# Four w_down products move from a stand-alone run into the first two Strassen pairs of a two-layer MLP

## The chip, the cores and the metric

The kernel runs on one core of one Trainium2 chip. The metric is device time in microseconds (us), the median of several runs; smaller is better. Traces come from one profiled execution.

## The reference

Two layers, each a token mixer (two kinds of attention with gates) followed by an MLP, on 512 tokens of width 1024 in float32. The change lies in the MLP of each layer:

```python
h = rmsnorm(x, norm_mlp)
return x + jnp.square(jax.nn.relu(h @ w_up)) @ w_down      # w_up 1024x4096, w_down 4096x1024
```

The result is a sum over the 4096 hidden columns, so a part of `w_down` can be applied as soon as its hidden columns are there.

## The kernel before

**Matmuls.** Every float32 operand is split into a rounded part `h` and a rest `lo`. A product with a contraction of 128 is three matmuls: h*h, h*lo, lo*h (lines 212 to 214, and 1195 through `mm`). Weights come from HBM as a tile `raw` (128x1024), ScalarE (ACT) casts it to `wh` (L186), VectorE (DVE) subtracts to get `wl` (L187).

**The MLP** (`mlp`, L912) holds the activations transposed, 128 columns by 512 tokens each, and has four stages:

1. The first 8 of 32 column blocks of `w_up` are multiplied plainly and give `acts[0:8]` (`PLAIN = 8`, L947 to L961).
2. A stand-alone run of w_down products (L963). One such product, a "down", is `down(c, m, w)` (L929): 4 activations by one 128-wide block of `w_down`, 12 matmuls of 512 columns, and one DVE addition into `x[m]` (L933). Downs come from the generator `D` in fixed order, c = 0 to 5 and m = 0 to 7; two successive ones share one `raw` tile from the array `wd2`, so tile k serves downs 2k and 2k+1. There are 48 of them in a layer; 16 stand here.
3. Twelve "units", one for each remaining pair g = 4 to 15 of `w_up` blocks (L975). A unit (`Strassen.unit`, L1203) does its 2x2 block product with seven products instead of eight. Each is 12 matmuls of 256 columns (`product`, L1190). The list in L975 says how many downs may go between a unit's products; the places are after products 1, 3, 5 and 6 (`between`).
4. The last quarter of `w_down` (`wdn`).

**Inside a unit** seven products p0 to p6 use four PSUM banks. p4 is added onto the bank of p2, p5 onto that of p0, p6 onto that of p1. So p4 waits until DVE has read p2 (`sub(y[:, 1], ...)`, shown as L1218), and p6 until DVE has read p1 (`c2`, L1236), which itself needs p4. After that the results go through ACT (ReLU, square, cast: L1259 to L1261) and GpSimd (POOL, L1262) to become two more activations.

**Conversion.** `S.load(g)` (L1157) fetches a pair's two raw tiles, into the buffers tagged `e` for even g and `raw` for odd g, two buffers each. `convert(g)` (L1167) forms four sums (two on POOL, L1176 and L1177; two on DVE, L1181 and L1182) and seven pairs `sh` (ACT, L1185) and `sl` (DVE, L1186), one for each product. Unit g carries along the conversion of pair g+1, and there are 8 buffers for `sh`, so a later `sh` waits for an earlier product to end.

**What sets the order.** Each engine works its own queue strictly in order; a scheduler fixes these queues when the program is built, by program order, readiness and free buffers. DMA loads of weights all go through one in-order queue on SyncE (SP). `order` (L678) lists the order and the buffer tag of the weight loads: a `wd2` tile with c = 0 or 1 (tiles 0 to 7, downs 0 to 15) uses the two `raw` buffers, which odd pairs also use; all later ones use the one buffer `crs`. One weight tile is converted ahead of its use (`ahead`, L199), and only when a `wh` buffer (there are two) is free of the products that read it.

The code that the change touches:

Of the kernel before, what the change touches and what calls it, by code (L numbers as in the profile page):

```python
# [137 lines left out]
def run(*gens):  # L138
    for g in gens:
        for _ in g:  # L140
            pass


class Body:
# [533 lines left out]
    def order(self, l):  # L678

        a = self.a  # L680
        flat = lambda ap: ap.rearrange("p k c -> p (k c)")
        wb = [flat(a["wb"][l, i]) for i in range(32)]
        for c in range(4):
            s = a["wva"][l, c]
            if l == 0 and c == 0:
                yield from ((s[:, j], 512) for j in range(2))
            else:
                yield flat(s), 1024
        yield from ((flat(a["wg2"][l, c]), 576) for c in range(4))
        for i in (0, 1, 2, 3, 8, 9, 4, 5, 6, 7, 10, 12, 13, 11):  # L690
            yield wb[i], 1024
        wo = [[flat(a["wo"][l, f, m]) for m in range(4)] for f in range(2)]
        for m in range(8):
            yield wb[16 + m], 1024
            if m % 2 == 1:
                yield wo[0][m // 2], 1024
            if m in (1, 3):
                yield wb[14 + m // 2], 1024
        yield from ((wb[24 + m], 1024) for m in range(8))
        yield from ((wo[1][m], 1024) for m in range(4))  # L700
        yield from ((flat(a["wout"][l, m]), 1024) for m in range(8))
        yield from ((flat(a["wup"][l, j]), 1024) for j in range(self.PLAIN))
        yield from ((a["wd2"][l, c, m], 1024, *(("crs",) if c > 1 else ())) for c in range(6) for m in range(4))
        yield from ((flat(a["wdn"][l, m]), 1024, *(("crs",) if m == 0 else ())) for m in range(8))

    def layer(self, l, u):
# [205 lines left out]
    def mlp(self, l, x, u, acc, gm):  # L912

        nc, a = self.nc, self.a
        R = None
        pend = []
        acts = []

        def act(ps):
            t = self.t("tmp", [128, T])  # L920
            nc.vector.scalar_tensor_tensor(t, ps, 0.0, R, op0=OP.max, op1=OP.mult)
            h = self.t("oh", [128, T], F32R)
            lo = self.t("ol", [128, T], F32R)
            nc.scalar.activation(t, t, AF.Square)
            nc.scalar.copy(h, t)
            nc.vector.tensor_tensor(lo, t, h.bitcast(F32), op=OP.subtract)
            acts.append((h, lo))

        def down(c, m, w):  # L929

            ps = self.bank()
            yield from self.gemm(ps, w, 4 * (m % 2), acts[4 * c:4 * c + 4], ks=4)
            nc.vector.tensor_add(x[m], x[m], ps)  # L933

        def downs():
            for c in range(6):
                for m in range(8):
                    if m % 2 == 0:
                        w = self.weights(a["wd2"][l, c, m // 2])
                    yield lambda: run(down(c, m, w))  # L940

        S = Strassen(self, l, x, gm)
        D = downs()
        raws = [None] * 16
        g0 = self.PLAIN // 2
        S.load(g0)
        for j in range(self.PLAIN):  # L947
            ps = self.bank()
            w = self.weights(a["wup"][l, j].rearrange("p k c -> p (k c)"))
            run(self.gemm(ps, w, 0, u))  # L950
            if R is None and j == 0:
                pend.append(ps)
                continue
            if R is None:
                R, _ = self.rstd(acc, (self.turn_tag(), self.turn_tag()))
                prep = S.prepare(R)
                for p in pend:
                    act(p)
            act(ps)
            for _ in range(3):  # L960
                next(prep, None)  # L961
        conv = S.convert(g0)
        for i in range(16):  # L963
            next(D)()
            if i < 7:
                next(prep, None)
                next(prep, None)
            elif i == 7:
                run(prep)
            else:  # L970
                next(conv, None)
            if i == 14:
                S.load(g0 + 1)
        run(conv)
        for g, n in zip(range(g0, 16), (0, 0, 3, 3, 4, 4, 4, 4, 4, 4, 2, 0)):  # L975
            S.load(g + 2)
            S.unit(g, D, n, acts)
        u_next = []
        acts = acts[24:]
        if l + 1 < L:  # L980
            acc = []
            self.load_small(l + 1)
            for m in range(8):
                ps = self.bank()
                w = self.weights(a["wdn"][l, m].rearrange("p k c -> p (k c)"))
                run(self.gemm(ps, w, 0, acts))
                nc.vector.tensor_add(x[m], x[m], ps)
                acc = self.sumsq(x[m], acc, m == 7)
                u_next.append(self.make_u(x[m], self.gain[:, 16 * l + 16:16 * l + 24], m))
                nc.scalar.dma_start(self.xs[m], x[m])  # L990
        else:
            self.last(x, acts, a["wdn"][l])
        self.acc = acc
        return u_next
# [305 lines left out]
```

## Time and profile before

| | |
|---|---|
| median of 3 runs | 1565.65 us (1564.94 to 1565.85) |
| the profiled execution's own time | 1566.34 us |
| its span, first to last instruction | 1564.5 us |
| TensorE (PE) busy in the span | 1541.8 us |
| VectorE (DVE) busy | 1079.2 us |
| ScalarE (ACT) busy | 775.3 us |
| GpSimd (POOL) busy | 206.8 us |
| mean granted TensorE clock | 0.994 |

PE counts as busy while matmuls stand in its pipeline. A timeline row has the start and the length in us, the engine, the line, the operation, what it writes and reads, and in brackets how long the engine sat idle before it and on what. A row of the view by windows has, for a stretch of the span, its length, then for PE, PE's weight loads, DVE, ACT and POOL the busy time and the number of instructions, then the granted clock (1.00 is full), the share of the DMA engines, and GB/s.

### The profile page before, as it was taken

To read this page: it belongs to the slowest core of one execution; us is meant where nothing else is said; L and a number is where in the kernel's file an instruction comes from. 1 tells how busy PE (TensorE), PEld (TensorE's weight loads), DVE (VectorE), ACT (ScalarE), POOL (GpSimd) and SP (SyncE) were. 2 spreads that over 40 slices of the span, in tenths; PEclk is the share of its full clock that TensorE was granted. 3 is DMA by queue.
4 is the path that set the end of the run, shared out by engine and by line. 5 is a ranking of instruction groups with operands and counts; after the bars stand their busy time and mean duration, and the time that the engine had idled before them with its cause. 6 is when DMAs were issued, how large, how long until landed. Compare 5 with 4: busy or idle time off the path is not lost. (4 is left out here: it accounts for less than half of the span.)

```text
span 1564.5 us, 22738 instructions
## 1 busy us (share of the span) xinstructions
PE 1541.8 (99%) x8460; PEld 1312.6 (84%) x8460; DVE 1079.2 (69%) x2204; ACT 775.3 (50%) x1455; POOL 206.8 (13%) x177
## 2 busy tenths in 40 slices
PE   9999999999999899999999999999999998999997
PEld 8867888888888899999887688888888888999997
DVE  5687988866478776664646689887574977766643
ACT  6444665543454455444443456555444625545552
POOL 4000000000200332221300000000002013222122
PEclk9999999999999999999999999999999999999998
DMA  7545422143333332322535543222433332333231
GB/s 239 169 134 153 118 82 81 60 131 96 105 94 122 95 95 94 109 81 65 181 109 172 158 129 95 71 78 68 148 95 95 95 121 82 102 101 96 67 96 54
DMA packets 56638, 169.57 MB, mean 108 GB/s; under 512 B 7344, under 2 KB 8112, under 8 KB 56528
## 3 DMA queue, kind: packets, MB, share of 16 engines
q1 hardware_dynamic: 53072, 161.84, 33.8%
q10 hardware_dynamic: 3456, 6.29, 1.2%
q8 instruction: 66, 1.08, 0.3%
q14 instruction: 44, 0.36, 0.1%
HBM read 140.77 MB, written 4.19 MB: 93 GB/s over the span
## 5 line engine op out<-in xcount | busy, mean ns | idle before, releaser
L186 ACT CAST wh<-raw 128x1024 fp32r<-128x1024 f32 (+2 forms) x187 | 192.6, 1030 | 279.1 <-issue 58.5
L187 DVE TENSOR_TENSOR wl<-raw,wh 128x1024 fp32r<-128x1024 f32 (+2 forms) x187 | 226.6, 1212 | 50.9 <-ACT wh L186 50.2
L212 PE MATMUL ps_mm<-uh,wh 128*128 128x512 f32 x512 | 205.2, 401 | 0.0
L214 PE MATMUL ps_mm<-uh,wl 128*128 128x512 f32 x512 | 202.3, 395 | 0.0
L213 PE MATMUL ps_mm<-ul,wh 128*128 128x512 f32 x512 | 202.1, 395 | 0.0
L399 ACT ACTIVATE E<-E,mx 128x128 f32<-128x128 f32 x192 | 108.0, 563 | 82.3 <-DVE mx L398 75.1
L430 ACT CAST pth<-ps_PT 128x512 fp32r<-128x512 f32 x144 | 73.0, 512 | 94.9 <-PE ps_PT L421 94.6
L212 PEld LDWEIGHTS ps_mm<-uh,wh 128*128 128x128 f32 x512 | 96.2, 188 | 26.6 <-issue 10.6
L214 PEld LDWEIGHTS ps_mm<-uh,wl 128*128 128x128 f32 x512 | 96.2, 188 | 20.4 <-issue 0.8
L213 PE MATMUL ps_mm<-ol,wh 128*128 128x512 f32 (+1 forms) x288 | 111.4, 387 | 1.2 <-POOL ol L1262 1.2
L212 PE MATMUL ps_mm<-oh,wh 128*128 128x512 f32 (+1 forms) x288 | 111.8, 388 | 0.0
L214 PE MATMUL ps_mm<-oh,wl 128*128 128x512 f32 (+1 forms) x288 | 111.2, 386 | 0.0
L398 DVE CUSTOM_DVE_ANT_0 E<-ps_S,ct 128x128 f32<-128x128 f32 x192 | 92.3, 484 | 26.5 <-PE ps_S L395 25.2
L213 PEld LDWEIGHTS ps_mm<-ul,wh 128*128 128x128 f32 x512 | 96.5, 188 | 15.1
L1186 DVE TENSOR_TENSOR sl<-s,sh 128x512 fp32r<-128x512 f32 x96 | 80.8, 845 | 35.7 <-ACT sh L1185 35.7
L431 DVE TENSOR_TENSOR ptl<-ps_PT,pth 128x512 fp32r<-128x512 f32 x144 | 85.1, 596 | 27.6 <-ACT pth L430 27.1
L1262 POOL TENSOR_TENSOR ol<-c,oh 128x512 fp32r<-128x512 f32 x48 | 62.7, 1306 | 284.3 <-ACT oh L1261 265.8
L1185 ACT CAST sh<-raw 128x512 fp32r<-128x512 f32 x72 | 44.6, 620 | 100.0 <-PE ps_S L1195 44.2
L253 POOL TENSOR_TENSOR acc<-sq 128x512 f32<-128x512 f32 (+1 forms) x6 | 8.3, 1391 | 594.4 <-DVE wl L187 580.2
L1185 ACT CAST sh<-s 128x512 fp32r<-128x512 f32 x96 | 59.3, 620 | 55.0 <-PE ps_mm L1195 19.2
L421 PE MATMUL ps_PT<-ct,E 128*128 128x128 f32 x480 | 83.0, 273 | 1.4 <-DVE ptl L431 1.4
L421 PEld LDWEIGHTS ps_PT<-ct,E 128*128 128x128 f32 x480 | 60.1, 140 | 14.8 <-DVE ptl L431 4.1
(441 smaller groups left out, 4085.0 us busy)
## 6 DMA issues: line engine op xcount, KB each, us to landing
raw<-wb SPq DMA_DIRECT2D x64, 512.0 KB, 3.3
raw<-wup SPq DMA_DIRECT2D x64, 512.0 KB, 3.6
raw<-wd SPq DMA_DIRECT2D x48, 512.0 KB, 3.6
kd<-hl SPq DMA_DIRECT2D x48, 256.0 KB, 4.6
w<-w SPq DMA_DIRECT2D x32, 256.0 KB, 5.7
q<-hl SPq DMA_DIRECT2D x64, 128.0 KB, 2.9
raw<-wo SPq DMA_DIRECT2D x16, 512.0 KB
raw<-wout SPq DMA_DIRECT2D x16, 512.0 KB, 3.5
```

Source lines behind the costliest of these rows:

```text
L186: nc.scalar.copy(h[:, :n], raw[:, :n])
L187: nc.vector.tensor_tensor(lo[:, :n], raw[:, :n], h[:, :n].bitcast(F32), op=OP.subtract)
L212: mm(ps, h[:, c], xh, start=start and i == 0, stop=False)
L213: mm(ps, h[:, c], xl, start=False, stop=False)
L214: mm(ps, lo[:, c], xh, start=False, stop=stop and i == ks - 1)
L398: nc.vector.tensor_tensor_reduce(e, ps[:, :n], self.mask[:, T - n:], -1.0, BIG, OP.add, OP.min, mx)
L399: nc.scalar.activation(e, e, AF.Exp, bias=mx, scale=-1.0, accum_out=sm[:, i:i + 1])
L421: nc.tensor.transpose(ps[:, j * 128:(j + 1) * 128], E[i][:, b * 128:(b + 1) * 128], self.ident)
L430: nc.scalar.copy(h[:, o:o + n], ps[:, :n])
L431: nc.vector.tensor_sub(lo[:, o:o + n], ps[:, :n], h[:, o:o + n].bitcast(F32))
L1185: nc.scalar.copy(h, src)
L1186: nc.vector.tensor_tensor(lo, src, h.bitcast(F32), op=OP.subtract)
```

## The change

Twelve downs instead of 16 stand in stage 2. The two steps of pair g=4's conversion that went beside each of downs 8 to 15 go two by two beside downs 8 to 11. The load of the second pair (g=5) is asked for at down index 10 instead of 14. Units g=4 and g=5 get two downs each instead of none. The tiles 6 and 7 of `wd2` (downs 12 to 15) move from the tag `raw` to `crs`. From the third unit on, the number of downs done is the same as before. Both layers run this code.

```diff
-        yield from ((a["wd2"][l, c, m], 1024, *(("crs",) if c > 1 else ())) for c in range(6) for m in range(4))
+        yield from ((a["wd2"][l, c, m], 1024, *(("crs",) if 4 * c + m > 5 else ())) for c in range(6) for m in range(4))
...
-        for i in range(16):
+        for i in range(12):
             next(D)()
             if i < 7:
                 next(prep, None)
...
                 run(prep)
             else:
                 next(conv, None)
-            if i == 14:
+                next(conv, None)
+            if i == 10:
                 S.load(g0 + 1)
         run(conv)
-        for g, n in zip(range(g0, 16), (0, 0, 3, 3, 4, 4, 4, 4, 4, 4, 2, 0)):
+        for g, n in zip(range(g0, 16), (2, 2, 3, 3, 4, 4, 4, 4, 4, 4, 2, 0)):
             S.load(g + 2)
             S.unit(g, D, n, acts)
```

## The prediction

> **What bounds the kernel now.** I read the page first, then the waits of PE, then PE's timeline around them, and last a table by windows.
>
> ```profile
> span 1564.5 us, 22738 instructions
> PE 1541.8 (99%) x8460; PEld 1312.6 (84%) x8460; DVE 1079.2 (69%) x2204; ACT 775.3 (50%) x1455; POOL 206.8 (13%) x177
> ```
>
> PE is the bound: 1541.8 of 1564.5 us. The change leaves every matmul in place, so it can only win what PE stands still or runs slowly. In the Strassen units of both layers these five rows of PE's timeline are the only ones with an idle time:
>
> ```profile
> 524.54 0.38 PE L1195 MATMUL ps_mm<-t,sh 128*128 128x256 f32 x1 [0.95 <-DVE y L1218]
> 529.65 0.39 PE L1195 MATMUL ps_O<-b_q,sh 128*128 128x256 f32 x1 [1.38 <-DVE c L1236]
> 542.18 0.39 PE L1195 MATMUL ps_O<-b_q,sh 128*128 128x256 f32 x1 [2.19 <-DVE c L1236]
> 1296.38 0.39 PE L1195 MATMUL ps_PT<-t,sh 128*128 128x256 f32 x1 [1.88 <-DVE y L1218]
> 1313.98 0.58 PE L1195 MATMUL ps_S<-b_q,sh 128*128 128x256 f32 x1 [2.19 <-DVE c L1236]
> ```
>
> All five lie in the first two units of a layer, the ones without downs, at p4 (L1218) or p6 (L1236). Now the windows: the stand-alone downs, the first two units of layer 0, the third and fourth, the eleventh unit, g=14 (two downs), the first two units of layer 1, and three short stretches behind the long waits.
>
> ```profile
> 474.16:517.68 43.52, 43.52 (x193) 36.04 (x192) 34.51 (x50) 15.48 (x22) 5.13 (x4) 1.00 0.34 110
> 517.68:546.05 28.37, 23.85 (x181) 23.23 (x180) 22.07 (x31) 15.61 (x29) 9.53 (x7) 0.94 0.37 113
> 546.05:584.00 37.95, 37.95 (x254) 34.99 (x253) 25.60 (x37) 20.63 (x37) 12.19 (x9) 1.00 0.28 87
> 708.90:724.83 15.93, 15.81 (x111) 14.62 (x109) 8.78 (x14) 6.51 (x12) 0.00 (x0) 1.00 0.34 102
> 1288.58:1317.83 29.25, 25.18 (x182) 24.71 (x180) 21.64 (x31) 15.16 (x29) 9.32 (x6) 0.88 0.36 109
> 542.20:545.80 3.60, 3.60 (x18) 3.60 (x19) 2.45 (x5) 2.39 (x5) 0.00 (x0) 0.54 0.48 146
> 1296.40:1299.90 3.50, 3.50 (x18) 3.50 (x19) 3.41 (x3) 0.62 (x1) 2.41 (x2) 0.57 0.57 180
> 1313.90:1317.30 3.40, 3.32 (x15) 3.32 (x16) 2.01 (x5) 1.83 (x4) 0.00 (x0) 0.50 0.56 154
> ```
>
> The first row gives a down: 192 matmuls in 43.52 us are 0.227 each, 2.72 for twelve. The price of a Strassen matmul stands in two neighbours:
>
> ```profile
> 530.95 0.28 PE L1195 MATMUL ps_O<-b_hl,sh 128*128 128x256 f32 x1
> 531.07 0.28 PE L1195 MATMUL ps_O<-b_q,sl 128*128 128x256 f32 x1
> ```
>
> They start 0.12 apart, so a product takes 12 x 0.12 = 1.44 and a unit 7 x 1.44 = 10.08. From p0 of the first unit to p1 of the third are 15 products, 21.60 us. The trace needs 28.37 in layer 0 and 29.25 in layer 1: **6.77 and 7.65 are lost, 14.42 together.** The waits are not all of it: after each wait of about 2 us the clock falls to 0.50 to 0.57 for some 3.5 us. Those three windows hold 18, 18 and 15 matmuls, which at 0.12 would take 2.16, 2.16 and 1.80 instead of 3.60, 3.50 and 3.32: 4.30 us in all. The rest is the waits, each with a slow first matmul behind it (0.38 against 0.28).
>
> **Why PE waits there.** Around the first unit of layer 0:
>
> ```profile
> 517.10 6.21 SPq L170 DMA_DIRECT2D raw<-wd  x2
> 520.65 1.05 ACT L186 CAST wh<-raw 128x1024 fp32r<-128x1024 f32 x1 [7.38 <-PE ps_O L1195]
> 521.73 1.23 DVE L187 TENSOR_TENSOR wl<-raw,wh 128x1024 fp32r<-128x1024 f32 x1 [2.86 <-ACT wh L186]
> 537.79 1.74 POOL L1177 TENSOR_TENSOR s<-raw 128x512 f32<-128x512 f32 x1
> 538.30 1.77 DVE L1186 TENSOR_TENSOR sl<-s,sh 128x512 fp32r<-128x512 f32 x1
> 542.37 0.69 DVE L1186 TENSOR_TENSOR sl<-s,sh 128x512 fp32r<-128x512 f32 x1
> ```
>
> ACT stands 7.38 us before the cast of tile 9. The row names PE as the releaser, but PE's product had long ended; the tile's load was issued only at 517.10. The casts of the next pair queue behind it; DVE then has them in a burst. And beside POOL's sum (537.79 to 539.53) a DVE subtraction takes 1.77 instead of the 0.69 at 542.37. The subtraction that frees PE's bank stands in that queue. A unit without downs gives DVE 10.08 us of cover; its work there is 22.07 / 2 = 11.0.
>
> **The change, part by part.** *PE.* Four downs, 4 x 2.72 = 10.88 us, leave the stand-alone run and enter the units: no matmul is added or saved, 0. In the changed program as built, PE has p0 p1 down p2 p3 down p4 p5, half of the next unit's p0, p6; every engine's order is the old one from the third unit's p1 on, and layer 1 has the same sequence with the banks exchanged. So the cover of a unit grows from 10.08 to 15.52. DVE's 11.0 gains two additions (0.69, as the other full-width steps) and a weight split (1.23): 13.6, below 15.52.
>
> *The earlier start.* The units now begin where down 12 began. What must be ready?
>
> ```profile
> 495.40 0.68 DVE L1186 TENSOR_TENSOR sl<-s,sh 128x512 fp32r<-128x512 f32 x1
> 506.80 0.39 PE L212 MATMUL ps_PT<-oh,wh 128*128 128x512 f32 x1
> 494.91 3.69 SPq L170 DMA_DIRECT2D raw<-wd  x2
> 503.68 5.77 SPq L1164 DMA_DIRECT2D raw<-wup  x2
> 512.85 1.29 POOL L1176 TENSOR_TENSOR s<-raw 128x512 f32<-128x512 f32 x1 [28.13 <-DMA raw<-wup]
> 514.17 1.76 DVE L1181 TENSOR_TENSOR s<-s,raw 128x512 f32<-128x512 f32 x1 [1.04 <-POOL s L1176]
> 501.34 1.06 ACT L186 CAST wh<-raw 128x1024 fp32r<-128x1024 f32 x1 [4.34 <-PE ps_O L213]
> ```
>
> Pair 4 is converted at 495.40 + 0.68 = 496.1, 10.7 before 506.80: the squeezed steps of its conversion cost 0. Pair 5's two loads take the places of tiles 6 and 7 in SP's queue, behind pair 6's loads as before: issued at 494.9 and 498.3 (3.69 less one issue of 0.33 later). The second was issued at 509.12 before (503.68 + 5.77 - 0.33) and released POOL at 512.85, 3.73 later; now it lands at 502.0, 4.8 before the units, as before (512.85 against 517.68). Tile 6 goes into `crs` early, as tile 8 did:
>
> ```profile
> L170 SPq DMA_DIRECT2D raw<-wd x48: 327/328/328, 244.2 to 1460.7; - x48
> ```
>
> The first load from `wd2` is issued at 244.2, long before the MLP; 0. *The added wait* is tile 7's: it needs `crs` back from tile 6. DVE's queue has L1181 of pair 5 ahead of that split: 502.0 + 1.29 on POOL + 1.76 + 1.23 for the split gives 506.3, and with 3.7 for the load 510.0. ACT's cast of tile 7 waits for it from 502.4 (the last row's end) on, and behind it stand pair 5's casts and the copy of p0 that p4's release needs. I walk on from 510.0: cast 1.05, split 1.23, a first `sl` 0.69; POOL's next sums can start only now, so another `sl` and one addition get the slowed 1.77 each; with 0.41 for the release of p2 that ends at 516.9. p4 starts at 506.80 + 4 x 1.44 + 2 x 2.72 = 518.0, so 1.1 us of cover are left; beyond them p4 waits one for one. Taken: 0.
>
> *p6 of both units.* The chain is: the second down's last L213 frees `wh`; cast, split, p4's release, one `sl`, `c2`. The third unit has it:
>
> ```profile
> 506.78 1.05 ACT L186 CAST wh<-raw 128x1024 fp32r<-128x1024 f32 x1 [4.38 <-PE ps_S L213]
> 555.84 1.05 ACT L186 CAST wh<-raw 128x1024 fp32r<-128x1024 f32 x1 [1.97 <-PE ps_O L213]
> 559.00 0.41 DVE L1236 TENSOR_TENSOR c<-y,ps_O 128x256 f32<-128x256 f32 x1
> ```
>
> The cast begins 0.02 before the down's end (506.78 against 506.80), so the down ended at 555.86 and `c2` 3.55 later. p6 may then start 3.6 after the down; in the new order it is due after p4, p5 and six matmuls, 2 x 1.44 + 0.72 = 3.60. So it is a dead heat: 0 to 0.5, taken 0.2 a unit. The unit g=14 agrees: 15.93 measured against 15.52.
>
> *What is late next: down 16 in the third unit.* Its last quarter needs the second activation of the second unit. Behind p6 of the first unit, at full clock, that took:
>
> ```profile
> 534.84 1.29 POOL L1262 TENSOR_TENSOR ol<-c,oh 128x512 fp32r<-128x512 f32 x1 [1.05 <-ACT oh L1261]
> ```
>
> 531.07 to 536.13 is 5.06. PE gets there in 0.12 + 0.72 + 1.44 + 10 x 0.227 = 4.55. The half clock hid this before; now PE waits 0.5, plus 0.1 for the slow restart: 0.65 a layer (0 to 1.0).
>
> **Sum.** Left in each layer: 2 x 0.2 + 0.65 = 1.05. Gain 14.42 - 2.10 = 12.3. The profiled execution took 1566.34, 0.69 above the median: 1566.34 - 12.3 - 0.7 = **1553.3 us**.
>
> [...]
>
> **The rivals.**
> - *A long wait stays.* POOL's sums slow DVE in the second unit too (1.77 against 0.69), and p6 has no cover. One wait like 542.18's costs 2.19 + 0.1 and about 1.43 of half clock, 3.7: 1557.0 with one, 1560.7 with one in each layer. For it: the dead heat. Against: third and fourth unit (37.95 busy of 37.95) run with the same POOL work without loss. 12%.
> - *Nothing is won.* Tile 7 puts ACT at the same lateness against the units as tile 9 did (510.0 - 506.80 = 3.2; 520.65 - 517.68 = 3.0), so if the waits come of that alone and the downs do not cover it, all return: 1562.5 to 1568.8. 6%.
> - *The slow clock has a cause of its own.* Then only the waits go: 1553.3 + 4.3 = 1557.6. All three stretches directly following a wait speak against it. 4%.
> - *Slower: tile 7 through `crs`.* Its load stands behind four others in SP's queue and ACT's queue behind it. p4 has 1.1 us; what lands later is paid by PE, and at some 2 us the half clock adds 1.4. To lose 3.1 us (0.2%) on top of the 12.3 it must cost 7.7 a layer, so land 1.1 + 7.7 - 1.4 = 7.4 us later than reckoned: 1569 and more. Its buffer and the queue ahead of it have rows that say otherwise. 8%, with what I do not see.
> - *The change does not do what it says:* the built order shows that it does, 0.
>
> **How the numbers follow.** The forecast has 70%: 1551.2 (14.42 gained) to 1555.5. Up to 1558.5 come the single long wait and the third rival, some 82% together. About 0.2% (3.1 us) is what a measurement can tell. Faster: 70 + 12 + 4 = 86%; within: 6%; slower: 8%.
>
> **What would show it.** Right: the two units take 32.5 + about 0.4 from p0 to p1 of the third, at clock 1.00; no L1218 or L1236 wait of PE over 0.6; a wait for L1262 of about 0.5 in down 16. Wrong: a window below 0.9 clock in the units; PE waiting for L1218 behind ACT's L186; waits in the third to eleventh unit.

## The result and the profile after

The changed kernel takes **1553.31 us** (median of 4 runs, 1552.85 to 1553.73) against 1565.75 (4 runs, 1564.94 to 1566.15) for the kernel before on the same chip: ratio 0.9921, 95% interval 0.9904 to 0.9938. The profiled execution took 1552.95 us. In the profile of the changed kernel every line after 971 is one higher than in that of the kernel before; the runs below shift them likewise. The page of the changed kernel:

```profile
span 1551.2 us, 22739 instructions
PE 1536.4 (99%) x8460; PEld 1306.6 (84%) x8460; DVE 1075.2 (69%) x2204; ACT 776.0 (50%) x1455; POOL 205.2 (13%) x177
```

The span is 13.3 us shorter with the same 8460 matmuls. The view by windows of the changed kernel, from p0 of the first unit to p1 of the third, layer 0 and layer 1:

```profile
506.86:539.61 32.75, 32.75 (x230) 30.69 (x228) 24.65 (x37) 17.17 (x30) 8.48 (x6) 1.00 0.38 122
1271.81:1304.56 32.75, 32.75 (x229) 30.68 (x228) 24.53 (x36) 17.17 (x30) 8.48 (x6) 1.00 0.38 121
```

Both layers take 32.75 us, without idle time and at full clock. Fifteen products at 1.44 and four downs at 2.72 are 32.48, so 0.27 is lost in each layer, where 6.77 and 7.65 were lost before. In the view of PE's waits of the changed kernel (total us, times, longest) no row names the releases L1219 and L1237 any more; the units have only these:

```profile
PE ps_mm L213 <- POOL ol L1263: 1.5, 2, 1.1
PE ps_PT L213 <- POOL ol L1263: 0.4, 1, 0.4
```

The 1.1 belongs to the end of the last unit, as the 1.2 did before. What is left, 0.4 in each layer, is the wait of down 16 in the third unit; PE's timeline of the changed kernel, layer 0:

```profile
543.12 0.39 PE L212 MATMUL ps_mm<-oh,wh 128*128 128x512 f32 x1
543.88 0.50 PE L213 MATMUL ps_mm<-ol,wh 128*128 128x512 f32 x1 [0.38 <-POOL ol L1263]
544.22 0.40 PE L214 MATMUL ps_mm<-oh,wl 128*128 128x512 f32 x1
```

The three starts lie 0.76 and 0.34 apart instead of 0.227: 0.53 and 0.11, together 0.65 us; layer 1 has the same. The timelines of SP, ACT, DVE and POOL around the first unit of the changed kernel show the steps on which the forecast stood:

```profile
506.32 6.22 SPq L170 DMA_DIRECT2D raw<-wd  x2
...
509.88 1.05 ACT L186 CAST wh<-raw 128x1024 fp32r<-128x1024 f32 x1 [7.44 <-PE ps_O L1196]
...
512.10 1.28 DVE L1187 TENSOR_TENSOR sl<-s,sh 128x512 fp32r<-128x512 f32 x2
512.87 1.68 POOL L1177 TENSOR_TENSOR s<-raw 128x512 f32<-128x512 f32 x1 [8.26 <-DVE sl L1187]
513.31 0.68 DVE L933 TENSOR_TENSOR x<-x,ps_mm 128x512 f32<-128x512 f32 x1
514.11 0.42 DVE L1219 TENSOR_TENSOR y<-y,ps_S 128x256 f32<-128x256 f32 x1
514.50 1.30 POOL L1178 TENSOR_TENSOR s<-raw 128x512 f32<-128x512 f32 x1
514.64 1.71 DVE L1187 TENSOR_TENSOR sl<-raw,sh 128x512 fp32r<-128x512 f32 x1
...
521.23 0.41 DVE L1237 TENSOR_TENSOR c<-y,ps_O 128x256 f32<-128x256 f32 x1
```

Tile 7's load is issued at 506.32 and its cast begins at 509.88 (forecast 510.0). The release of p2 ends at 514.53, 3.6 us ahead of p4 (518.10). Note which DVE steps POOL's sums slow: not the addition into `x` at 513.31 and not the release at 514.11, which read PSUM while POOL works, but the `sl` at 514.64 (1.71 instead of 0.69), whose two inputs both lie in SBUF. It began behind POOL's sum of 514.50. The two `sl` steps of 512.10 kept their time; there the sum that began during the second of them was the one stretched (1.68 instead of 1.29).

### The profile page after: what moved, and what is told of

Read it like the earlier page. It is cut to its first block, busy times and chain, and to the rows that moved or that the text cites. A ratio compares the mean times of both kernels' runs of the same rounds, so it can differ in the third digit from the quotient of the medians.

```text
span 1551.2 us, 22739 instructions
## 1 busy us (share of the span) xinstructions
PE 1536.4 (99%) x8460; PEld 1306.6 (84%) x8460; DVE 1075.2 (69%) x2204; ACT 776.0 (50%) x1455; POOL 205.2 (13%) x177
## 3 DMA queue, kind: packets, MB, share of 16 engines
q8 instruction: 66, 1.08, 0.3%
## 4 chain that ended last, share of the span: by engine, by line
PE 95%; DVE 3%; ACT 1%; issue 1%; POOL 0%; DMA 0%; DVEq 0%; SPq 0%; POOLq 0%; ACTq 0%
PE ps_mm L212 12%; PE ps_mm L213 12%; PE ps_mm L214 12%; PE ps_S L1196 4%; PE ps_O L1196 4%; PE ps_O L447 4%; PE ps_mm L1196 3%; PE ps_PT L421 3%; PE ps_PT L1196 3%; PE ps_S L212 3%; PE ps_S L213 3%; PE ps_S L214 3%; PE ps_PT L212 3%; PE ps_PT L213 3%; PE ps_PT L214 3%; PE ps_O L212 3%
## 5 line engine op out<-in xcount | busy, mean ns | idle before, releaser
L187 DVE TENSOR_TENSOR wl<-raw,wh 128x1024 fp32r<-128x1024 f32 (+2 forms) x187 | 226.6, 1212 | 49.8 <-ACT wh L186 48.9
L1187 DVE TENSOR_TENSOR sl<-s,sh 128x512 fp32r<-128x512 f32 x96 | 76.6, 801 | 36.6 <-ACT sh L1186 36.3
```

What stands on the lines that cost most here:

```text
L187: nc.vector.tensor_tensor(lo[:, :n], raw[:, :n], h[:, :n].bitcast(F32), op=OP.subtract)
L1187: nc.vector.tensor_tensor(lo, src, h.bitcast(F32), op=OP.subtract)
```

## The experiments

The theory of the prediction: DVE's work in a unit without downs (11.0 us) does not fit the cover of 10.08, and the downs give it cover. Its chief rival: the loads decide, tile 9's or pair 5's, whatever the cover. A third theory came up on the way: DVE's 11.0 is so long only because of POOL. "Before" in this section is the kernel before on the chip of the run, 1564.87 to 1565.13 us in the median.

**One part of the change at a time.** First all downs moved, but tiles 6 and 7 in `raw` as before, which puts pair 5's load behind them:

```diff
...
-  (("crs",) if 4 * c + m > 5 else ())
+  (("crs",) if c > 1 else ())
...
-            if i == 10:
+            if i == 11:
```

> Only the downs move (12 alone, two in each of the first two units); tiles 6 and 7 stay in the raw buffers and the second pair's load stays behind them. If the cover that the downs give decides, the gain stays: 1552 to 1556 us, first two units of a layer at about 32.5 us and full clock. If the earlier loads decide, pair 5 lands at 512.9 as before, now 6 us into the first unit, its casts come in the second unit and the long waits return there: 1559 to 1566 us.

Measured: 1564.31 us, ratio 0.9996 (0.9987 to 1.0005). **Nothing is won**: as long as POOL makes the sums, both parts are needed. DVE, POOL and PE in the first unit of this run (layer 0):

```profile
513.33 1.30 POOL L1177 TENSOR_TENSOR s<-raw 128x512 f32<-128x512 f32 x1 [28.14 <-DMA raw<-wup]
...
514.66 1.77 DVE L1182 TENSOR_TENSOR s<-s,raw 128x512 f32<-128x512 f32 x1 [0.87 <-POOL s L1177]
517.28 1.67 DVE L1183 TENSOR_TENSOR s<-s,raw 128x512 f32<-128x512 f32 x1
520.08 1.78 DVE L1187 TENSOR_TENSOR sl<-s,sh 128x512 fp32r<-128x512 f32 x1
522.56 0.68 DVE L933 TENSOR_TENSOR x<-x,ps_O 128x512 f32<-128x512 f32 x1
524.30 0.42 DVE L1219 TENSOR_TENSOR y<-ps_S,y 128x256 f32<-128x256 f32 x1
525.23 0.41 DVE L1237 TENSOR_TENSOR c<-y,ps_O 128x256 f32<-128x256 f32 x1
...
525.70 0.39 PE L1196 MATMUL ps_O<-b_q,sh 128*128 128x256 f32 x1 [3.43 <-DVE c L1237]
```

Pair 5 lands at 513.3, 6 us into the units. Its conversion stands in DVE's queue ahead of a down's addition and the release, and three of its steps take 1.7 instead of 0.69. p6 of the first unit waits 3.43 (layer 1: 3.3), longer than any wait of PE in the units before. I had expected the waits in the second unit; they came in the first, because the late conversion meets the unit that carries it. Then the other half, the loads alone, sixteen downs standing alone:

```diff
...
-  (("crs",) if c > 1 else ())
+  (("crs",) if 4 * c + m > 5 else ())
...
                 next(conv, None)
+                next(conv, None)
-            if i == 14:
+            if i == 10:
```

> Only the loads move (tag crs for tiles 6 and 7, pair 5 asked for at index 10); 16 downs stand alone and the first two units have none. If the cover decides, the waits at L1218 and L1236 stay: 1561 to 1567 us, the two units between 25 and 29.5 us a layer instead of 21.6 without loss. If late loads were the cause, most of the 14.4 us goes: 1552 to 1556 us.

Measured: 1566.36 us, ratio 1.0008 (0.9999 to 1.0018). The loads alone win nothing. PE's waits in this run:

```profile
PE ps_O L1196 <- DVE c L1237: 2.2, 1, 2.2
PE ps_S L1196 <- DVE c L1237: 2.2, 1, 2.2
PE ps_PT L1196 <- DVE y L1219: 1.9, 1, 1.9
PE ps_mm L1196 <- DVE y L1219: 1.8, 1, 1.8
```

One wait of about 2 us in each of the four units; before, the first unit of layer 0 had two shorter ones.

**Cover in doses.** Two downs in the first unit alone, in the second alone, and one in each; 14 downs stand alone, tile 7 goes into `crs` and pair 5's load is asked for at index 12 (the first of the three; the others have 0, 2 and 1, 1 in the list):

```diff
...
-  (("crs",) if 4 * c + m > 5 else ())
+  (("crs",) if 4 * c + m > 6 else ())
...
-        for i in range(12):
+        for i in range(14):
...
-            if i == 10:
+            if i == 12:
...
-        for g, n in zip(range(g0, 16), (2, 2, 3, 3, 4, 4, 4, 4, 4, 4, 2, 0)):
+        for g, n in zip(range(g0, 16), (2, 0, 3, 3, 4, 4, 4, 4, 4, 4, 2, 0)):
```

> 14 downs alone, two in the first unit, none in the second (tile 7 through crs, pair 5 asked for at index 12). The first units lose 2.9 and 3.7 us in the two layers of before, the second ones 4.0 and 4.0. If each unit's loss comes of its own missing cover, the first unit's 6.6 us go but for 0.2 and the second's stay: 1559 to 1560.5 us, with two half-clock stretches left. If the loads or a burst carried over from the first unit decide, the second unit's waits shrink too: below 1556 us.

Measured: 1559.72 us, ratio 0.9966 (0.9952 to 0.9979). PE's timeline shows the covered first unit with 0.1 at p6 and the second with its old wait (layer 1 has the same):

```profile
540.50 0.38 PE L1196 MATMUL ps_O<-b_q,sh 128*128 128x256 f32 x1 [2.33 <-DVE c L1237]
```

> 14 downs alone, none in the first unit, two in the second. If each unit's loss comes of its own missing cover, the second units' 8 us go but for 1.5 (p6 and the activation that the third unit waits for), the first units' stay: 1558.5 to 1560.5 us, with one half-clock stretch left (layer 1). If a late load for the first unit is all of it, little is won, over 1563 us, or the wait moves into the second unit.

Measured: 1559.25 us, ratio 0.9962 (0.9947 to 0.9976). Here the second unit is clean and the first has its two waits:

```profile
518.88 0.38 PE L1196 MATMUL ps_PT<-t,sh 128*128 128x256 f32 x1 [0.81 <-DVE y L1219]
523.98 0.39 PE L1196 MATMUL ps_S<-b_q,sh 128*128 128x256 f32 x1 [1.38 <-DVE c L1237]
```

> One down in each of the first two units (fourteen alone), tile 7 in crs, pair 5's load at the twelfth. Cover of a unit 10.08 + 2.72 = 12.8 us against DVE's 11.0 + 0.69 for a down's addition (and a split of 1.23 in places). Theory A (the waits are DVE work that does not fit beside a unit's products, paid one for one beyond the cover): 12.8 holds all but a few tenths of it, so both units lose at most 0.5 each and the time is 1554 to 1557. Theory B (what counts is when pair 5's load lands against the units' start, as e1 suggests): it lands one place later in SP's queue, about 5 us after its place in the changed kernel and the units start 2.7 us later each, so waits of 1 to 2.5 us come back in one unit of each layer and the time is 1558 to 1561, as with two downs in one unit alone.

Measured: 1554.84 us, ratio 0.9935 (0.9921 to 0.9948). One down a unit already brings 10.3 of the 12.4 us; p6 of the second unit waits 0.3 and no other release shows in PE's waits. So, with pair 5's load early, the waits are paid per unit and shrink with the unit's cover, whichever unit has it.

**POOL's sums.** Nothing of the change, only the two POOL sums of a conversion left out (two products take plain quarters of the weights in their place, so part of the computation is missing):

```diff
-        G.tensor_tensor(s1, a21, a22, op=OP.add)
-        G.tensor_tensor(s3, a11, a21, op=OP.add)
...
+        s1, s3 = a21, a11
...
```

> The kernel before, with POOL's two sums of the weight conversion left out (the two products take plain quarters in their place, so this leaves out part of the computation). No down is moved. Theory A (POOL's sums, beside which a DVE subtraction takes 1.77 instead of 0.69, make DVE late in the units without downs): four DVE steps a pair get shorter by up to 1 us each, which takes DVE's 11.0 us a unit below the cover of 10.08, so the waits of the first two units go or shrink below 0.6 and the time is 1553 to 1557. Theory B (ACT's cast of tile 9 behind its load is late by itself): the waits stay at 1 to 2.2 us and the time is 1562 to 1566.

Measured: 1554.02 us, ratio 0.9930 (0.9916 to 0.9943). Without a single down in the units most of the gain is there: POOL's sums made DVE late. This run takes away the slowing and the wait for the sums' results together. Then the same sums, made by DVE itself, in the kernel before:

```diff
-        G = nc.gpsimd
-        G.tensor_tensor(s1, a21, a22, op=OP.add)
-        G.tensor_tensor(s3, a11, a21, op=OP.add)
...
+            if i == 1:
+                nc.vector.tensor_tensor(s1, a21, a22, op=OP.add)
+            if i == 4:
+                nc.vector.tensor_tensor(s3, a11, a21, op=OP.add)
```

> The kernel before, the two sums of a pair's conversion made by DVE (each at its place before the first use) instead of POOL; nothing is left out and no down is moved. Theory A (POOL's sum costs DVE more, 1.77 against 0.69 for the step beside it, than the 0.69 that DVE would need for the sum itself): DVE gains about 2 x (1.08 - 0.69) = 0.8 us a unit, which brings 11.0 to about the cover of 10.08, so most of the waits go and the time is 1553.5 to 1558, near the 1554.0 without the sums. Theory B (only the amount of DVE's work against the cover counts): DVE has 1.4 us a unit more, the waits grow and the time is 1566 to 1572.

Measured: 1555.07 us, ratio 0.9935 (0.9922 to 0.9947), the full computation. The groups of DVE's `sl` steps in the first two units of layer 0, kept apart by shape (count, busy us, mean ns); first the kernel before:

```profile
L1186 DVE TENSOR_TENSOR sl<-s,sh 128x512 fp32r<-128x512 f32 x8 | 8.1, 1027 | 1.7 <-ACT sh L1185 1.7
L1186 DVE TENSOR_TENSOR sl<-raw,sh 128x512 fp32r<-128x512 f32 x6 | 6.0, 995 | 0.1
```

The same groups with the sums on DVE:

```profile
L1187 DVE TENSOR_TENSOR sl<-s,sh 128x512 fp32r<-128x512 f32 x8 | 5.5, 685 | 1.7 <-ACT sh L1186 1.7
L1187 DVE TENSOR_TENSOR sl<-raw,sh 128x512 fp32r<-128x512 f32 x6 | 4.1, 683 | 0.1
```

And the windows of those two units with the sums on DVE:

```profile
517.74:540.65 22.91, 22.18 (x181) 21.72 (x180) 19.46 (x34) 15.16 (x28) 2.61 (x2) 1.00 0.39 114
1283.63:1306.35 22.72, 22.06 (x181) 21.73 (x180) 19.46 (x34) 15.09 (x28) 2.61 (x2) 1.00 0.38 114
```

Fourteen `sl` steps take 9.6 us instead of 14.1. DVE's work in two units falls from 22.07 to 19.46 although it does four sums more (0.6 of the fall is an addition of a stand-alone down that now ends before the window): 9.7 a unit, under the cover of 10.08. The 28.37 us of layer 0 become 22.91, 1.3 above the 21.60 of pure products; 0.7 of that is a wait of PE for ACT's `sh`. Over the whole span DVE's busy time *rises* from 1079.2 to 1090.7: the 24 sums of layer 0 take 19.6 us (the first of a pair 0.94 in the mean, the second 0.69), and if layer 1 is alike 39.2 are added and 27.7 of that come back from steps that POOL no longer slows. By this estimate a POOL sum had cost DVE 0.58, less than the 0.82 of doing it. The share of the span would have argued against this edit; the stretch argues for it.

In the first unit the gain came in part through the load that the prediction named. `crs` is one buffer, so tile 9's load waits for the split (L187) of tile 8. The kernel before, and then the run with the sums on DVE:

```profile
515.86 1.21 DVE L187 TENSOR_TENSOR wl<-raw,wh 128x1024 fp32r<-128x1024 f32 x1
```

```profile
513.91 1.22 DVE L187 TENSOR_TENSOR wl<-raw,wh 128x1024 fp32r<-128x1024 f32 x1
515.16 6.26 SPq L170 DMA_DIRECT2D raw<-wd  x2
```

Before, that split stands behind the addition of 514.17, which waits 1.04 us for POOL's sum and takes 1.76. With the sums on DVE it comes 1.95 us earlier, and so, within 0.1, do the load (515.16 against 517.10) and the cast of tile 9 (518.76 against 520.65). The second unit has no such load: there DVE works with hardly a pause from 535.11 to p6's release, and two `sl` steps in a row take 1.78 and 1.77.

The run in which the moved downs won nothing, with the sums on DVE, tells whether its late load was a cause of its own:

> The run with the old buffers and load place (tiles 6 and 7 in raw, pair 5's load at the eleventh down, so that it lands some 6 us after the units begin), where the four downs in the units won nothing, with the two sums of the conversion on DVE. Theory A (POOL's sums beside DVE are the cause, and the late load only gathers the slowed steps into the first unit): the first unit's p6 waits under 1 us in place of 3.4, and the time is 1553 to 1557. Theory B (a load that lands inside the units is late by itself: all conversion of pair 5 stands ahead of p4's and p6's releases, whoever does the sums): the waits of 2 to 3 us stay and the time is 1560 to 1565.

Measured: 1553.55 us, ratio 0.9925 (0.9909 to 0.9942). The same DVE steps as quoted above, with the same late load (this kernel's lines are one higher still):

```profile
514.51 0.69 DVE L1183 TENSOR_TENSOR s<-s,raw 128x512 f32<-128x512 f32 x1
516.04 0.69 DVE L1184 TENSOR_TENSOR s<-s,raw 128x512 f32<-128x512 f32 x1
519.05 0.68 DVE L933 TENSOR_TENSOR x<-x,ps_O 128x512 f32<-128x512 f32 x1
519.65 0.69 DVE L1188 TENSOR_TENSOR sl<-s,sh 128x512 fp32r<-128x512 f32 x1
521.39 0.42 DVE L1220 TENSOR_TENSOR y<-ps_S,y 128x256 f32<-128x256 f32 x1
522.32 0.42 DVE L1238 TENSOR_TENSOR c<-y,ps_O 128x256 f32<-128x256 f32 x1
```

The first addition runs at the same time (514.51 against 514.66), but `c2` at 522.32 instead of 525.23: 2.9 us of the 3.43 that p6 waited, though the cast of the down's tile came later (519.15 against 518.54). No wait of PE for a release is left. The load is late only together with the slowed steps.

**What is left.** The third unit's first place for a down is left empty, so that down 16 comes one product later:

```diff
+        skip = [g == 6]
...
-            if next(todo, None) is not None:
+            if skip[0]:
+                skip[0] = False
+            elif next(todo, None) is not None:
```

> The changed kernel with the third unit's first place for a down left empty, so that its downs follow one product later and the first of them reaches its last quarter 1.44 us later. Theory A (PE's 0.65 in down 16 is the wait for the second unit's second activation alone, 0.54 late): it goes, in both layers, and the time is 1552.0 (1551.5 to 1552.6), about 1.3 us below the changed kernel. Theory B (the third unit then lacks cover ahead of p4 or p6, as the units without downs did): a wait for a DVE step of up to 1 us takes its place and the time is 1553 to 1555.

Measured: 1552.33 us (5 runs, 1551.79 to 1552.75), ratio 0.9919 (0.9905 to 0.9932). Its third and fourth unit:

```profile
540.03:577.90 37.87, 37.87 (x253) 34.92 (x252) 27.49 (x38) 21.32 (x38) 12.47 (x9) 1.00 0.30 94
```

No idle time is left there, so the wait was the activation's alone. The median is 1.0 us below the changed kernel's and the span 0.9, but the two ratios lie within each other's intervals: the trace shows the gain, the times do not settle it. With this edit and the sums on DVE together:

> The changed kernel with both: the third unit's first place for a down left empty, and the two sums on DVE. Theory A (the first two units have their cover, and what is left there is p6's 0.1 a unit): the downs' cover and the sums on DVE are two ways to the same gain, so they do not add up, and the time is 1551.5 to 1552.6, within 0.5 us of the changed kernel with the empty place alone (1552.3). Theory B (DVE's work beside POOL also slows units elsewhere): a further 0.5 to 2 us goes, 1550.3 to 1551.8.

Measured: 1552.42 us, ratio 0.9917 (0.9904 to 0.9931). The two remedies do not add up; they mend the same lateness. These two are the best versions I ran.

**Which waits halve the clock.** The prediction tied the half clock to waits of about 2 us (1.88 and 2.19 in its rows). The two runs at 2.3 and 1.4 us above (one part of the downs) have none at all, so I put chains of multiplications by one ahead of `c2` in the units g = 8 to 13 of the changed kernel:

```diff
+        for _ in range({8: 12, 9: 15, 10: 18, 11: 21, 12: 24, 13: 30}.get(g, 0)):
+            V.tensor_scalar(y[:, 0], y[:, 0], 1.0, None, op0=OP.mult)
         V.tensor_tensor(c2[:, 256:], y[:, 0], p5, op=OP.add)
```

> The changed kernel with a chain of 12, 15, 18, 21, 24 and 30 multiplications by one in place of y ahead of the c2 step of the units g = 8 to 13 of both layers, so that PE waits ahead of p6 for times that grow from unit to unit (from nothing to some 6 us, or more). Only the profile is read: which waits are followed by a granted clock near 0.5 for some 3.5 us. Theory A (a threshold of about 1.8 us, as the prediction put it): every wait of 1.9 us or more is followed by a slow stretch, none below is. Theory B (a window that runs by itself, in which the wait has to fall): waits of 1.5 to 4 us are followed by one or not, without an order in their length, and the longest always are.

Measured: the added waits at p6 were at most 1.1 us, shorter than meant, and no stretch at half clock followed (mean granted clock 0.998). It decides nothing above that. So once more, with longer chains:

> As the run with added waits, which gave waits of 0.2 to 1.3 us and no slow stretch behind any of them; the chains are now 18, 24, 24, 24, 28 and 34 long in units g = 8 to 13, so that the waits of p6 come to some 1.5 to 3.5 us, up to twelve of them. Theory A (a threshold near 1.8 us, as the prediction put it): a stretch at a granted clock near 0.5 stands behind each wait of 1.9 us or more. Theory B (a wait has to meet a window that runs by itself): behind some of them, in no order of their length.

Measured: PE stood idle for 1.06, 1.86, 2.29, 2.69 and 4.90 us at the long waits of layer 0, and for 1.06, 1.86, 2.57, 2.80 and 5.13 in layer 1. Half clock follows those of 1.86, 2.69 and 4.90 (and 1.86, 2.80, 5.13), **not those of 2.29 and 2.57**. So length alone does not decide. The windows of this run, laid 3.41 us wide where the stretches at half clock begin and end:

```profile
647.26:650.68 3.42, 1.56 (x11) 1.10 (x10) 2.77 (x5) 0.55 (x1) 1.26 (x1) 1.00 0.00 0
650.68:654.09 3.41, 3.41 (x19) 3.41 (x18) 1.06 (x2) 2.39 (x5) 0.97 (x1) 0.50 0.00 0
671.16:674.57 3.41, 1.92 (x10) 1.44 (x8) 3.21 (x7) 0.00 (x0) 1.28 (x1) 1.00 0.00 0
674.57:677.98 3.41, 2.61 (x21) 2.61 (x22) 1.81 (x5) 2.26 (x4) 0.00 (x0) 1.00 0.00 0
698.46:701.88 3.42, 0.73 (x5) 0.27 (x3) 3.18 (x11) 1.33 (x2) 0.00 (x0) 1.00 0.00 0
701.88:705.29 3.41, 3.41 (x16) 3.41 (x17) 2.38 (x5) 1.96 (x4) 0.00 (x0) 0.50 0.15 16
```

The half clock lasts one such stretch (two at the longest wait, 1510.84 to 1517.66), and its beginnings lie whole multiples of 3.413 us apart (701.88 - 650.68 = 51.20 = 15 x 3.413; in the kernel before 1296.87 - 542.52 = 754.35 = 221 x 3.413). What counts is PE's idle time *within one stretch of this grid*: 3.42 - 1.56 = 1.86 idle, and the next runs at 0.50; the wait of 2.29 falls across a border, 1.49 and 0.80 idle, and nothing follows. The run with pair 5's late load shows it most clearly:

```profile
522.64:526.06 3.42, 0.36 (x3) 0.37 (x4) 3.42 (x8) 0.05 (x1) 0.00 (x0) 1.00 0.31 69
526.06:529.47 3.41, 3.41 (x19) 3.41 (x18) 2.28 (x4) 2.51 (x5) 0.09 (x1) 0.50 0.72 284
1290.64:1294.06 3.42, 1.64 (x14) 1.44 (x12) 3.33 (x4) 0.93 (x3) 0.59 (x1) 1.00 0.51 153
1294.06:1297.47 3.41, 1.85 (x15) 1.85 (x16) 3.25 (x8) 1.50 (x3) 0.00 (x0) 1.00 0.63 180
1297.47:1300.88 3.41, 3.41 (x24) 3.15 (x23) 1.64 (x3) 3.41 (x8) 1.37 (x2) 1.00 0.33 127
```

Of two waits of 3.4 and 3.3 us the first lies in one stretch (3.06 idle, then 0.50), the second falls into halves (1.78 and 1.56), and the clock stays at 1.00. Of the stretches of this grid that were read in the kernel before, in the runs with the late load and with the loads alone and in this one, away from the end of the span, every one with 1.86 us idle or more has half clock behind it and none with up to 1.56 has. Between them both occur: half clock behind one of 1.68 (1507.42 to 1510.84 of this run), none behind one of 1.71 (the loads alone) nor behind the 1.78. So the border lay near 1.7, half of the stretch. At the end of the span of the kernel before, one of 1.53 (1552.87 to 1556.28) has half clock behind it too.

**Not tried:** two `crs` buffers, which might take away the wait of tiles 7 and 9 for theirs.

## Why the prediction came out right, point by point

- **PE's loss as the whole prize:** right. Of the 14.42 lost in the two units, 0.27 a layer is left, and 0.65 a layer is new in the third unit. 14.42 - 1.84 = 12.6 of the span's 13.3 us. Of the rest, 0.5 comes in the last 15 us of the span (matmul by matmul the changed kernel is 12.8 us ahead where they begin and 13.3 where they end); the cause of that stays open.
- **The cover of 10.08 against 11.0, and 15.52 against 13.6:** the step holds (doses of 0, one and two downs gave 1566, 1555 and 1553 us), and DVE worked 24.65 / 2 = 12.3 a unit where I reckoned 13.6. But the 11.0 was no given amount of work. The prediction named the slowed 1.77 among the reasons, but took the 11.0 as fixed and gave POOL's part in it no price; leaving out POOL's sums won 11.1 us, and moving them to DVE 10.0, without any more cover.
- **"The earlier start", loads cost 0:** the cost was right, the weight was not. The early load of pair 5 is a condition of the gain: without it 1564.31. The prediction never asked what the time would be without that part of the change; it is 11 us more. With the sums on DVE the condition falls away (1553.55).
- **Tile 7's added wait, 0:** right. The cast at 509.88 was forecast at 510.0, and the release of p2 ended at 514.5, ahead of 516.9. The two steps that I slowed to 1.77 were not slow: the `sl` had begun before POOL's sum, and the addition (0.68) reads PSUM. The `sl` that was slow (1.71) came behind the release.
- **p6, 0.2 a unit:** 0.10 and 0.10, a restart without a wait: the dead heat was won.
- **Down 16, 0.65 a layer:** 0.65 in both layers, and it went when the down came later, with no other wait in its place.
- **The half clock after each wait of about 2 us:** it went with the waits, as forecast, so the 4.30 are in the sum. The reason given, the length of the wait, fell: waits of 2.33 in the run with downs in the first unit alone had no half clock behind them (1.00 over both units), one of 2.19 before had. What the traces show is a grid of 3.413 us, in which 1.86 idle of one stretch was enough for half clock in the next. The 4.30 is so that execution's own share; where the grid falls differs from trace to trace (its first border lies 3.2 us behind the start of the span in the kernel before, 0.4 in the run with pair 5's late load and 2.1 in the one with the longer waits). It is also a gross price; a slow stretch may hide a later wait, as at down 16 (no wait there before, 0.65 after): from p0 to the second unit's p1, layer 1's first unit with a slow stretch took 15.26 us, layer 0's without one 14.35, 0.9 apart where 1.34 (3.50 - 2.16) was reckoned.
- **The last term, 0.7 for the profiled execution's distance from the median:** counted in part twice, and that 1553.3 meets 1553.31 so closely is luck. That execution had three stretches at half clock (mean clock 0.994), which the 14.42 already holds; most other runs of the kernel before show a clock of 0.996 and took 1565.1 us in the mean, those with 0.998 took 1564.2. Without the term the sum is 1554.0. What made up for it are the 1.84 left in place of 2.10, and the 0.5 at the end of the span, which was not forecast.
- **The rivals:** the long wait (12%) showed up in the experiments, but not in this kernel. The slower case, tile 7 through `crs`, did not come.

What POOL's sums cost DVE stood in the rows: in the changed kernel `sl` from two SBUF tiles took 1.71 beside POOL's sum, the release with a PSUM input 0.42, and of a POOL sum and such an `sl` the one that began second was stretched (the `sl` at 514.64, the sum at 512.87). Had I priced it by the rows of before (1.77 - 0.69 = 1.08 a slowed step), POOL's sums would have stood in the prediction as the cause, not as one reason for a rival.

## What to carry to other kernels

When an engine "has too much work" in a stretch, compare the mean time of one form of its instructions inside and outside that stretch before you give it cover: a step of 1.77 beside another engine's work is a cost of that neighbour, and to take the work back from an idle engine can be cheaper than it looks. An edit that costs nothing may still be what the gain hangs on; ask of each part what comes back without it. Price a half clock by the idle time within one stretch of its grid, not by the length of a wait.

## What I had not expected of the hardware

- The half clock comes on a grid of 3.413 us: in the stretches read away from the end of the span the clock was 0.50 behind 1.86 us idle or more and 1.00 behind up to 1.56, and between 1.68 and 1.78 both occurred; behind the wait of 3.3 us across a border it stayed at 1.00.
- Beside a POOL sum of 1.29 us DVE steps with two SBUF inputs took up to 1.78 us instead of 0.69 (1.67 to 1.78 in the rows above), and a POOL sum was stretched itself (1.68 at 512.87); the DVE steps that read PSUM kept their 0.42 and 0.68 beside it.
- DVE did the second sum of a pair in 0.69 us, about half of POOL's 1.29 (the first, sometimes stretched to 1.7, took 0.94 in the mean).
